# A sparse expert block: the row lookup issued earlier, and other row counts for the gathers

## The chip, the cores and the metric

The kernel runs on one core of a Trainium2 chip. Its time is the device time of one execution in microseconds (us); lower is better. Three executions of the kernel before took 2243.35, 2243.98 and 2247.09 us, median 2243.98 us.

Five engines work side by side, each through its own queue of instructions in order: TensorE (PE in the profile; its weight loads are PEld), VectorE (DVE), ScalarE (ACT), GpSimd (POOL) and SyncE (SP). They wait for one another through semaphores. Transfers run on 16 DMA engines and are issued here by SP (weights) and by POOL (gathers and scatters).

## The reference

One decoder block on 1024 tokens of width 1024. Attention with a forget gate and a gated MLP come first; their merged output goes through a layer norm. Then comes a mixture of 32 experts, which takes most of the time here, and after it a gated embedding and two more norms. Cut to what matters:

```python
x = layer_norm(ALPHA * x + mix)
logits = x @ w_router + b_router            # 1024 x 32
top_val, top_idx = top_k(logits, 4)         # four experts a token
gates = softmax(top_val)
for e in range(32):                         # the rows of x that chose e
    gu = xb @ w_gu[e] + b_gu[e]             # 1024 -> 2048
    gate, up = min(gu[:, :1024], 7), clip(gu[:, 1024:], -7, 7)
    h = (up + 1) * (gate * sigmoid(1.702 * gate))
    y = h @ w_dn[e] + b_dn[e]               # 1024 -> 1024
ffn = sum over a token's four experts of gates * y
x = layer_norm(ALPHA * x + ffn)
```

All inputs are float32. The 4096 assignments spread unevenly over the experts.

## The kernel before, in words

**Row counts.** Experts are ranked by how many tokens chose them. An expert of rank r is given a fixed window of `WIN[r]` rows (lines 35 and 36), filled up with dummy rows; rows beyond a window go through a loop at the end (line 1485). `ORDER` (line 38) is the order in which the ranks are worked on: 32 places, called experts 0 to 31 below, with 120, 92, 232, 102, 98, 180, 114, 88, 256, 100, 128, 192, 118, 128, 150, 156, 124, 144, 164, 124, 134, 208, 108, 128, 176, 126, 138, 168, 120, 130, 160 and 104 rows. A window of over 128 rows is handled in two pieces, of 128 rows and the rest, each with a gather and a scatter of its own.

**The sequence.** Lines 1193 to 1199 write down the work in units, `seq`. Each expert has eight units of the first product: gate and up columns (`"g"`, `"u"`), numbered 0 to 3, in the order g0 g1 u0 u1 g2 g3 u2 u3. Behind the eight units of expert r come the four down-product units (`"d"`) of expert r - 1. So twelve units make a group, and the loop at line 1450 walks through them. Each unit uses 1 MB of float32 weights. For each unit the loop issues:

- the split of a later unit's weights into two half-precision parts: `high` on ScalarE (L1221, four units ahead) and `low` on VectorE (L1227, three units ahead, by the program's order), and then the load of a unit still further ahead on SP (`stage`, L121);
- the unit's own matmuls on TensorE, three for each pair of a 128 x 128 weight block and the rows: `s1` and `columns` (L1318 to L1320), or `s2` for the down product. A down product of at most 128 rows has the rows on the weights' side and 512 columns moving (L1396 to L1400); a wider one goes through `columns` and is transposed back;
- what is due by then from earlier units. `Pipe` (lines 46 to 66) holds these pieces: `p.at(k, f)` runs f at the start of the k-th unit from there.

**The lookup of an expert's rows.** `find(r)` (line 1269) builds a one-hot of the places with eight comparisons on VectorE (`onehot`, L1240). Two units later `pick` multiplies it with token numbers and gate values on TensorE (L1248), eight small matmuls for each 128 rows, and VectorE copies the result (L1250). One unit later `gather` (line 1254) makes the indices with three small VectorE instructions (L1260 to L1262) and issues the indirect DMA on GpSimd (L1265), which brings the rows from DRAM into a tile `xg`.

**The use of the rows.** In the units g2, g3, u2 and u3 of expert r, behind that unit's matmuls, `turn` (line 1280) transposes the rows of expert r + 1 on TensorE (L1288), four transposes each time: one piece in g2 and u2, a second piece in g3 and u3. One unit later ScalarE and VectorE split the result into two halves (L1293, L1294).

**Where the lookup is issued.** `find(r + 3)` stands in unit d0 of expert r (line 1462), the ninth of the twelve units of the group of expert r + 1. The gather goes out at the start of the twelfth unit, and the transposes stand behind the fifth unit of the next group. `find(1)` and `find(2)` are issued ahead of the loop and in its first unit.

**The scatter.** `put` (line 1366) scales an expert's output on ScalarE (L1371) and adds it to the result in DRAM with an indirect DMA on GpSimd (L1374), one or four units into the next group.

**Buffers.** `xg`, the one-hots, the products `z` and the outputs `y` take turns in 16 tiles (`t4`). Weights as loaded, weights as split, `xgT` and `hT` share 15 tiles (`t8`). PSUM's eight banks are handed out in turn too.

Of the kernel before, what the change touches and what calls it, by code (L numbers as in the profile page):

```python
# [30 lines left out]
OFF_V, OFF_U, OFF_GV, OFF_GA, OFF_GB = 1024, 1544, 2056, 2568, 3592  # L31


PICK_TILES, PICK = 4, 26
WIN = [120, 256, 232, 208, 192, 180, 176, 168, 164, 160, 156, 150, 144, 138, 134, 130, 128,
       128, 128, 126, 124, 124, 120, 118, 114, 108, 104, 102, 100, 98, 92, 88]

ORDER = [0, 30, 2, 27, 29, 5, 24, 31, 1, 28, 17, 4, 23, 16, 11, 10, 21, 12, 8, 20, 14, 3, 25, 18, 6, 19, 13, 7, 22, 15, 9, 26]

# [1125 lines left out]
def moe(k, windows, m, p):  # L1165
# [12 lines left out]
    pipe = Pipe()  # L1178
# [36 lines left out]
    def high(n):  # L1215
        if n < len(loads):
            if loads[n][0] == "d" and full(loads[n][1]):
                units[loads[n]] = staged.pop(n)
                return
            units[loads[n]] = k.t8([P, 2, KB // 2, 512], F16, "unit")  # L1220
            nc.scalar.activation(units[loads[n]][:, 0], staged[n], AF.Copy, scale=WS)  # L1221

    def low(n):
        if 0 <= n < len(loads):
            if n in staged:
                u = units[loads[n]]
                nc.vector.scalar_tensor_tensor(u[:, 1], staged.pop(n), WS, u[:, 0], op0=OP.mult, op1=OP.subtract)  # L1227
            stage(n + N_AHEAD)

    def win(r):  # L1230
        return [(w0, min(P, windows[r] - w0)) for w0 in range(0, windows[r], P)]
# [4 lines left out]
    def onehot(r, place):  # L1236
        W = windows[r]
        oh = k.t4([P, NB, 256], F16, "oh")
        for b in range(NB):
            nc.vector.tensor_scalar(oh[:, b, :W], k.iota1[:, :W], place(b), None, op0=OP.is_equal)  # L1240
        return oh

    def pick(r, oh, val):
        out = []
        for w0, n in win(r):
            ps = k.bank()
            for b in range(NB):
                nc.tensor.matmul(ps[:n, :4], oh[:, b, w0:w0 + n], val(b), start=b == 0, stop=b == NB - 1)  # L1248
            t = k.small([P, 4], FT, "slot_t", 4)
            nc.vector.tensor_copy(t[:n], ps[:n, :4])  # L1250
            out.append(t)
        return out
# [16 lines left out]
    def find(r, p):  # L1269

        if r >= R:
            return
        oh = onehot(r, lambda b: k.place[:, b, r:r + 1])

        def second():
            ts = pick(r, oh, lambda b: k.val[:, b, :, r])
            p.at(1, gather, r, ts)
        p.at(2, second)

    def turn(r, w0, n, h, p):  # L1280

        if r not in xgT:
            xgT[r] = k.t8([P, 2, KB, 256], F16, "xgT")
        t, x = xgT[r], xg[r, w0]
        pt = k.bank()
        for j in range(4):
            b = 4 * h + j
            nc.tensor.transpose(pt[:, j * P:j * P + n], x[:n, b * P:(b + 1) * P], k.identf[:n, :n])  # L1288
        src = pt.rearrange("p (j t) -> p j t", j=4)[:, :, :n]
        hi, lo = (t[:, s, 4 * h:4 * h + 4, w0:w0 + n] for s in range(2))  # L1290

        def fin():
            nc.scalar.activation(hi, src, AF.Copy, scale=16.0)  # L1293
            nc.vector.scalar_tensor_tensor(lo, src, 16.0, hi, op0=OP.mult, op1=OP.subtract)  # L1294
        p.at(1, fin)
# [26 lines left out]
    def s1(kind, r, u, p):  # L1322
        un = units.pop((kind, r, u))
        banks = chunks(kind, r, u)
        columns(r, u, un, xgT[r], banks)
        if u % 2:
            p.at(1, take, kind, r, u // 2, banks, p)
# [54 lines left out]
    def s2(r, u, p):  # L1382
        W = windows[r]
        un, h = units.pop(("d", r, u)), hT[r]
        kh = u % 2
        if u == 3:
            del hT[r]
        if W <= P:
            if kh == 0:
                yps[r] = k.bank()  # L1390
            ps = yps[r]
            o = ps[:W]
            for b in range(4):
                kb, start, stop = 4 * kh + b, kh == 0 and b == 0, kh == 1 and b == 3
                if full(r):
                    nc.tensor.matmul(o, h[:, kb, :W], un[:, b], start=start, stop=stop)  # L1396
                    continue
                nc.tensor.matmul(o, h[:, 0, kb, :W], un[:, 0, b], start=start, stop=False)
                nc.tensor.matmul(o, h[:, 0, kb, :W], un[:, 1, b], start=False, stop=False)
                nc.tensor.matmul(o, h[:, 1, kb, :W], un[:, 0, b], start=False, stop=stop)  # L1400
            if kh:
                p.at(1, put, r, 0, W, u // 2, ps)
            return
        banks = chunks("d", r, u)
        columns(r, u, un, h, banks)
        if kh == 0:
            return
        yt = [k.t2([P, 2, 256], FT, "yt") for _ in range(2)]

        def back():  # L1410
            for w0, n in win(r):
                pt = k.bank()
                for c in range(4):
                    nc.tensor.transpose(pt[:n, c * P:c * P + P], yt[c // 2][:, c % 2, w0:w0 + n], k.identf)
                p.at(1, put, r, w0, n, u // 2, pt)

        def out():
            for i in range(2):
                nc.scalar.activation(yt[i][:, :, :W], banks[i][:, :, :W], AF.Copy)
        p.at(1, out)  # L1420
        p.at(3, back)
# [28 lines left out]
    for n, (kind, r, u) in enumerate(seq):  # L1450
        pipe.tick()
        high(n + LEAD)
        if n:
            low(n + LEAD - 1)
        if n >= 30:
            next(over, None)
        if n == len(seq) - TAIL[7]:
            post_rows(k)
        if kind == "d":
            s2(r, u, pipe)  # L1460
            if u == 0:
                find(r + 3, pipe)
        else:
            s1(kind, r, u, pipe)
            if n == 0:
                over = rest()
            if r == 0 and (kind, u) == ("g", 0):
                find(2, pipe)
            if u >= 2 and r + 1 < R:
                i = 2 * (kind == "u") + u - 2  # L1470
                ws = win(r + 1)
                if i % 2 < len(ws):
                    turn(r + 1, *ws[i % 2], i // 2, pipe)
        if n < TAIL[9]:
            step(TAIL[10])
        if n == TAIL[9]:
            p.drain()
# [56 lines left out]
def post_rows(k):  # L1534

    k.bg = row_halves(k, k.a["b_ple_gate"], "bg")
    k.rows = {}
    for n in ("ln2_g", "ln2_b", "ln3_g", "ln3_b"):
        k.rows[n] = k.t4([P, D], FT, n)
        k.row(k.rows[n], k.a[n][0])  # L1540
# [114 lines left out]
@with_exitstack  # L1655
def block_kernel(ctx: ExitStack, tc: tile.TileContext, a: dict, out: bass.AP, dbg=None, phases=9, windows=None):
    ctx.enter_context(tc.manual_schedule())
    k = K(ctx, tc, a, out, dbg)
    windows = [(r, (windows or WIN)[r]) for r in ORDER]
    p = Pipe()  # L1660
    mT, uo = pre(k, p)
    if phases > 1:
        m = mid(k, mT, uo, windows, p)
    if phases > 2:
        us = moe(k, windows, m, p)
    if phases > 3:
        post(k, us, p)
# [24 lines left out]
```

## Time and profile before

| | |
|---|---|
| median of three runs | 2243.98 us |
| lowest, highest | 2243.35, 2247.09 us |
| the profiled execution | 2249.39 us, span 2247.7 us |
| TensorE busy | 2089.9 us, 93% of the span |
| VectorE busy | 1652.9 us, 74% |
| ScalarE busy | 1338.4 us, 60% |
| GpSimd busy | 438.6 us, 20% |
| moved by DMA | 528.77 MB, mean 235 GB/s |
| weights of the experts | 384 loads of 1 MB |
| gathers of rows | 47, 10.0 us median to landing |

The loop over the experts runs from about 764 to 2100 us of the span. A row of the list of instructions in order of time gives the start in us, the duration in us, the engine, the line, the operation, the tiles written and read, the shape and the count, and in brackets the idle time of the engine just before and what ended it. A row of a stretch of time gives the stretch, its length, busy time with the number of instructions in brackets for TensorE, its weight loads, VectorE, ScalarE and GpSimd, then the granted TensorE clock as a share of full speed, the mean busy share of the 16 DMA engines, and GB/s. Spans on GpSimd are rough.

### The profile page before, as it was taken

How to read it: one execution, taken by the hardware profiler on the slowest of the kernel's cores; microseconds unless marked ns; L12 is line 12 of the kernel's file. 1: busy time of each engine (PE TensorE's matmuls, PEld its weight loads, DVE VectorE, ACT ScalarE, POOL GpSimd, SP SyncE). 2: the span in 40 equal slices, each digit the busy share in tenths (PEclk: the TensorE clock that was granted, in tenths of full speed). 3: DMA queues.
4: the chain of work that ended last, by engine and by line, in shares of the span. 5: the costliest groups of instructions: out<-in, count | busy, mean ns of one | idle time of the engine just before them, and what ended most of it. 6: DMA issues, size and time to landing. Idle time of an engine off the chain costs nothing.

```text
span 2247.7 us, 54560 instructions
## 1 busy us (share of the span) xinstructions
PE 2089.9 (93%) x23096; PEld 1692.1 (75%) x23096; DVE 1652.9 (74%) x2705; ACT 1338.4 (60%) x1936; POOL 438.6 (20%) x360
## 2 busy tenths in 40 slices
PE   7999889999999888997999898998999999998596
PEld 6797555444488667977789797998989889998442
DVE  4677666333368786877698798898989888997666
ACT  3324555222111566776688687786978878887443
POOL 1000000000000221203212124221423142341154
PEclk9999999999999999998999999999999999999798
DMA  7201223222224798998989898999989999998621
GB/s 239 67 20 39 68 54 106 58 74 69 92 99 159 264 361 291 316 341 317 336 312 349 271 374 307 335 354 304 358 301 359 351 345 338 354 357 287 222 87 73
DMA packets 285512, 528.77 MB, mean 235 GB/s; under 512 B 16860, under 2 KB 66060, under 8 KB 285264
## 3 DMA queue, kind: packets, MB, share of 16 engines
q1 hardware_dynamic: 263840, 468.29, 59.7%
q0 software_dynamic: 21424, 56.96, 9.3%
q8 instruction: 182, 2.98, 0.5%
q14 instruction: 66, 0.54, 0.1%
HBM read 481.50 MB, written 37.38 MB: 231 GB/s over the span
## 4 chain that ended last, share of the span: by engine, by line
PE 65%; DMA 12%; issue 10%; DVE 6%; POOL 3%; ACT 3%; SPq 1%; ACTq 0%; POOLq 0%; DVEq 0%
PE bank L1318 10%; PE bank L1319 10%; PE bank L1320 10%; DMA xg<-h_dram,slot_i 10%; PE bank L211 3%; PE bank L210 3%; PE bank L209 3%; PE bank L223 3%; PE bank L225 3%; PE bank L224 3%; PE bank L1396 2%; PE bank L1288 1%; DVE unit L1227 1%; POOL rs_t L132 1%; PE bank L835 1%
## 5 line engine op out<-in xcount | busy, mean ns | idle before, releaser
L1227 DVE SCALAR_TENSOR_TENSOR unit<-stage,unit 128x2048 f16<-128x2048 f32 x376 | 853.5, 2283 | 47.3 <-ACT unit L1221 45.8
L1318 PE MATMUL bank<-xgT,unit 128*128 128x128 f16 (+27 forms) x4096 | 758.6, 227 | 0.0
L1320 PE MATMUL bank<-xgT,unit 128*128 128x128 f16 (+27 forms) x4096 | 757.6, 227 | 1.0 <-issue 1.0
L1319 PE MATMUL bank<-xgT,unit 128*128 128x128 f16 (+27 forms) x4096 | 757.9, 227 | 0.1
L1221 ACT ACTIVATE unit<-stage 128x2048 f16<-128x2048 f32 x376 | 715.2, 1910 | 46.0 <-DVE unit L1227 33.5
L1318 PEld LDWEIGHTS <-unit 128*128 128x128 f16 x5056 | 500.4, 99 | 7.1 <-issue 1.7
L1319 PEld LDWEIGHTS <-unit 128*128 128x128 f16 x5056 | 500.1, 99 | 7.0 <-issue 1.6
L1320 PEld LDWEIGHTS <-unit 128*128 128x128 f16 x5056 | 500.0, 99 | 3.0 <-issue 0.5
L1265 POOL DMA_INDIRECT xg<-h_dram,slot_i x47 | 223.8, 4763 | 833.9 <-DVE slot_w L1260 352.2
L1337 ACT ACTIVATE z<-bank,bias 128x128 f32<-128x128 f32 (+27 forms) x512 | 155.6, 376 | 96.3 <-PE bank L1320 92.3
L1318 PE MATMUL bank<-hT,unit 128*128 128x232 f16 (+14 forms) x960 | 208.2, 238 | 0.0
L1320 PE MATMUL bank<-hT,unit 128*128 128x232 f16 (+14 forms) x960 | 208.0, 238 | 0.0
L1319 PE MATMUL bank<-hT,unit 128*128 128x232 f16 (+14 forms) x960 | 208.0, 238 | 0.0
L1294 DVE SCALAR_TENSOR_TENSOR xgT<-bank,xgT 128x512 f16<-128x512 f32 (+12 forms) x94 | 52.2, 556 | 151.0 <-ACT xgT L1293 150.3
L223 PE MATMUL bank<-xT,unit 128*128 128x512 f16 x384 | 145.5, 379 | 2.7 <-DVE pT L62 2.7
L225 PE MATMUL bank<-xT,unit 128*128 128x512 f16 x384 | 145.5, 379 | 1.6 <-DVE unit L104 1.6
L224 PE MATMUL bank<-xT,unit 128*128 128x512 f16 x384 | 145.5, 379 | 0.0
L1374 POOL DMA_INDIRECT acc_dram<-y,slot_i x47 | 120.5, 2564 | 113.0 <-ACT y L1371 100.3
L1288 PE MATMUL bank<-identf,xg 128*128 128x128 f32 (+25 forms) x376 | 54.8, 270 | 65.3 <-DMA xg<-h_dram,slot_i 65.3
L209 PE MATMUL bank<-unit,xT 128*128 128x256 f16 (+1 forms) x384 | 106.3, 277 | 3.3 <-ACT unit L103 3.3
L210 PE MATMUL bank<-unit,xT 128*128 128x256 f16 (+1 forms) x384 | 106.2, 276 | 2.1 <-DVE unit L104 2.1
L742 POOL DMA_DIRECT2D brow<-in_b_out_dram x1 | 0.5, 519 | 545.2 <-DVE unit L104 545.2
(384 smaller groups left out, 3644.9 us busy)
## 6 DMA issues: line engine op xcount, KB each, us to landing
stage<-in_w_gate_up_dram SPq DMA_DIRECT2D x256, 1024.0 KB, 11.1
stage<-in_w_down_dram SPq DMA_DIRECT2D x128, 1024.0 KB, 9.2
stage<-in_w_in_dram SPq DMA_DIRECT2D x22, 512.0 KB, 3.8
stack<-qk_tmp SPq DMA_DIRECT2D x96, 64.0 KB, 2.0
stage<-in_w_in_dram SPq DMA_DIRECT2D x5, 1024.0 KB
xs<-in_x_dram SPq DMA_DIRECT2D x8, 512.0 KB, 9.4
crow<-c_dram SPq DMA_DIRECT2D x8, 512.0 KB, 4.2
stage<-in_w_out_dram SPq DMA_DIRECT2D x4, 1024.0 KB, 5.1
```

Source lines behind the costliest of these rows:

```text
L209: nc.tensor.matmul(ps, lh, rh, start=b == 0, stop=False)
L210: nc.tensor.matmul(ps, lh, rl, start=False, stop=False)
L223: nc.tensor.matmul(box[0], lh, rh, start=b == 0, stop=False)
L224: nc.tensor.matmul(box[0], lh, rl, start=False, stop=False)
L225: nc.tensor.matmul(box[0], ll, rh, start=False, stop=b == n - 1)
L1221: nc.scalar.activation(units[loads[n]][:, 0], staged[n], AF.Copy, scale=WS)
L1227: nc.vector.scalar_tensor_tensor(u[:, 1], staged.pop(n), WS, u[:, 0], op0=OP.mult, op1=OP.subtract)
L1265: nc.gpsimd.indirect_dma_start(out=x[:n], out_offset=None, in_=k.h1d, in_offset=bass.IndirectOffsetOnAxis(ap=i[:n, :1], axis=0))
L1318: nc.tensor.matmul(o, wh, x[:, 0, kb, :W], start=start, stop=False, skip_group_check=True)
L1319: nc.tensor.matmul(o, wh, x[:, 1, kb, :W], start=False, stop=False, skip_group_check=True)
L1320: nc.tensor.matmul(o, wl, x[:, 0, kb, :W], start=False, stop=stop, skip_group_check=True)
L1337: nc.scalar.activation(zs[r][c // 2][:, k0 + c % 2, :W], banks[c // n][:, c % n, :W], AF.Identity, bias=bias_of(r, 4 * v + c + 4 * k0), sc ...
```

## The change

The lookup of expert r + 2 is issued in unit g2 of expert r, the fifth of its group, instead of the ninth (in the old numbering, `find(r + 3)` in d0 of expert r, which belongs to the group of r + 1; both look up the expert two ahead of the group). Expert 2 is still looked up in unit g0 of expert 0. Nine of the 32 windows grow, so that every piece of more than 80 rows has a divisor between 13 and 16; the sum of the windows goes from 4510 to 4538. Rows that are added are dummy rows or rows that went through the loop at the end before.

```diff
 PICK_TILES, PICK = 4, 26
 WIN = [120, 256, 232, 208, 192, 180, 176, 168, 164, 160, 156, 150, 144, 138, 134, 130, 128,
-       128, 128, 126, 124, 124, 120, 118, 114, 108, 104, 102, 100, 98, 92, 88]
+       128, 128, 126, 126, 126, 120, 120, 120, 112, 104, 104, 104, 98, 96, 90]
...
         if kind == "d":
             s2(r, u, pipe)
-            if u == 0:
-                find(r + 3, pipe)
         else:
             s1(kind, r, u, pipe)
             if n == 0:
                 over = rest()
-            if r == 0 and (kind, u) == ("g", 0):
-                find(2, pipe)
+            if (kind, u) == ("g", 2 if r else 0):
+                find(r + 2, pipe)
```

## The prediction

> **What bounds the kernel now.** I read the page first, then the list of waits of TensorE, then the same list cut to the expert loop, then single stretches.
>
> ```profile
> span 2247.7 us, 54560 instructions
> PE 2089.9 (93%) x23096; PEld 1692.1 (75%) x23096; DVE 1652.9 (74%) x2705; ACT 1338.4 (60%) x1936; POOL 438.6 (20%) x360
> PE 65%; DMA 12%; issue 10%; DVE 6%; POOL 3%; ACT 3%; SPq 1%; ACTq 0%; POOLq 0%; DVEq 0%
> ```
>
> TensorE is busy 93% of the span, so what it waits for is what can be won. Its waits, longest first (total us, times, longest), and then its waits on the gathered tile from 1020 to 2060 us alone:
>
> ```profile
> PE bank L1288 <- DMA xg<-h_dram,slot_i: 65.3, 12, 11.3
> PE bank L1584 <- DMA pl<-ple_dram: 22.0, 1, 22.0
> ...
>   DMA xg<-h_dram,slot_i: 53.9, 10
> ```
>
> One wait stands far above the rest: the transposes (L1288) of an expert's rows wait for their gather. 53.9 of the 65.3 us fall on ten experts of the running loop. The other two waits, 11.4 us together, belong to the first two experts. No row shows a wait of TensorE for a weight unit inside the loop; there it stops for gathers alone.
>
> The gathers' issues on GpSimd (start, us, the span on POOL), and the transposes that waited for them, for three experts:
>
> ```profile
> 1012.84 15.01 POOL L1265 DMA_INDIRECT xg<-h_dram,slot_i  x1 [39.40 <-DVE slot_g L1262]
> 1225.85 2.96 POOL L1265 DMA_INDIRECT xg<-h_dram,slot_i  x1 [22.38 <-issue]
> 2009.33 14.30 POOL L1265 DMA_INDIRECT xg<-h_dram,slot_i  x1 [22.64 <-issue]
> ...
> 1035.14 0.85 PE L1288 MATMUL bank<-identf,xg 88*128 88x88 f32 x4 [11.25 <-DMA xg<-h_dram,slot_i]
> 1250.05 1.05 PE L1288 MATMUL bank<-identf,xg 118*128 118x118 f32 x4 [6.81 <-DMA xg<-h_dram,slot_i]
> 2031.82 0.96 PE L1288 MATMUL bank<-identf,xg 104*128 104x104 f32 x4 [7.81 <-DMA xg<-h_dram,slot_i]
> ```
>
> From issue to release these took 1035.14 - 1012.84 = 22.3 us (88 rows), 24.2 us (118 rows) and 22.5 us (104 rows). Without its wait TensorE would have been at the transposes at 1023.9, 1243.2 and 2024.0, so the cover that the order gave was 11.1, 17.4 and 14.7 us. 24.2 us is the longest of the ten.
>
> **What a stall costs beside its idle time.** Eight stretches, the first seven us after a waiting transpose began (the column before the DMA share is the granted clock):
>
> ```profile
> 1035.10:1042.10 7.00, 6.96 (x83) 6.96 (x84) 4.83 (x6) 4.06 (x8) 0.00 (x0) 0.59 0.32 86
> 1250.00:1257.00 7.00, 6.95 (x49) 6.63 (x50) 5.24 (x6) 3.50 (x5) 0.00 (x0) 0.58 0.27 99
> 1372.50:1379.50 7.00, 7.00 (x81) 6.78 (x82) 4.97 (x7) 5.13 (x9) 0.00 (x0) 0.80 0.48 112
> 1416.30:1423.30 7.00, 6.96 (x77) 6.91 (x78) 5.19 (x6) 4.84 (x8) 0.00 (x0) 0.76 1.02 351
> 1541.20:1548.20 7.00, 6.97 (x64) 6.92 (x65) 5.19 (x6) 4.04 (x8) 0.00 (x0) 0.66 0.76 268
> 1666.10:1673.10 7.00, 7.00 (x78) 7.00 (x79) 5.79 (x6) 5.52 (x8) 0.00 (x0) 1.00 0.59 159
> 1828.20:1835.20 7.00, 7.00 (x84) 6.96 (x85) 3.39 (x5) 3.69 (x5) 0.00 (x0) 0.68 0.95 285
> 2031.80:2038.80 7.00, 6.98 (x60) 6.96 (x61) 5.41 (x6) 3.67 (x7) 0.00 (x0) 0.59 0.32 81
> ```
>
> After the longer stalls TensorE runs at a reduced clock. The shortfalls from 1.00 are 0.41, 0.42, 0.20, 0.24, 0.34, 0, 0.32 and 0.41, in sum 2.34; times 7 us that is 16.4 us. I take 15, since matmuls that wait for their weights' load lose less than the clock does.
>
> Do the others use a stall to get ahead? Mostly not. From 850 to 2060 us:
>
> ```profile
> ACT xgT L1293 <- PE bank L1288: 79.3, 31, 10.8
> ...
> DVE xgT L1294 <- ACT xgT L1293: 138.8, 49, 11.9
> ...
> SPq L121 <- PE bank L1288: 131.5, 23, 16.1
> ...
> ACT unit L1221 <- DMA stage<-in_w_gate_up_dram: 4.7, 6, 2.1
> ```
>
> ScalarE's queue has the copy of the transposed rows at its head, VectorE waits for ScalarE, and the weight loads wait for buffers. Everything stops for up to 10.8 to 16.1 us, and everything moves up when the stall goes. ScalarE waited 4.7 us in all for gate and up weights, so the loads have room.
>
> **The change, part by part.**
>
> *The lookup moves up.* Its pieces are eight one-hot comparisons on VectorE, the pick (8 small matmuls per 128 rows on TensorE), three slot operations on VectorE and the indirect DMA on GpSimd. The same work is issued four units of the sequence earlier: the gather goes out behind the eighth unit of a group of twelve instead of the twelfth. So it gains the four down-product units between. These take at least this for a narrow expert (the span, TensorE's busy time and matmuls):
>
> ```profile
> 1265.60:1276.15 10.55, 10.55 (x58) 4.91 (x57) 10.48 (x19) 9.57 (x10) 0.00 (x0) 1.00 0.96 335
> ```
>
> The covers become 11.1 + 10.55 = 21.6, 17.4 + 10.55 = 28.0 and 14.7 + 10.55 = 25.2 us, against landings of 22.3, 24.2 and 22.5. At most 0.7 us would be left, for the first. On POOL's queue the scatters of the previous expert come behind the gather before and after, and nothing is passed; the buffers' rotation keeps its slack, as far as I count the allocations. Removed: 53.9 us of waits and 15 us of slow clock. Bounds: 69.6 us with the first expert's remainder kept, 53.9 + 16.4 = 70.3 us without; where the cover doesn't grow at all is a rival below.
>
> *Where it moves to costs something.* TensorE's pick now stands ahead of the seventh unit, and it waits for the one-hot, which VectorE can start only behind the weight unit it makes in that step. For a narrow expert VectorE is just in time. Group 9 (100 rows), VectorE, then TensorE's two transposes around the sixth and seventh unit, then the one-hot where it stands now; below, VectorE's fourth unit and the transposes ahead of the seventh in group 29, the last with a lookup:
>
> ```profile
> 1153.53 8.89 DVE L1227 SCALAR_TENSOR_TENSOR unit<-stage,unit 128x2048 f16<-128x2048 f32 x4
> 1162.34 0.26 DVE L1354 TENSOR_SCALAR z<-z 128x200 f32<-128x200 f32 x1
> ...
> 1158.47 0.66 PE L1288 MATMUL bank<-identf,xg 128*128 128x128 f32 x4 [0.35 <-DMA xg<-h_dram,slot_i]
> 1163.20 0.62 PE L1288 MATMUL bank<-identf,xg 128*128 128x128 f32 x4
> ...
> 1174.32 1.52 DVE L1240 TENSOR_SCALAR oh<-iota,place 128x192 f16<-128x192 f16 x8
> ...
> 1983.03 2.29 DVE L1227 SCALAR_TENSOR_TENSOR unit<-stage,unit 128x2048 f16<-128x2048 f32 x1 [0.64 <-ACT unit L1221]
> ...
> 1989.72 0.43 PE L1288 MATMUL bank<-identf,xg 32*128 32x32 f32 x4
> ```
>
> VectorE ends its fourth unit at 1162.4, so the one-hot would end at 1162.4 + 1.5 = 1163.9. TensorE reaches the seventh unit halfway between the transposes, near 1161.1, and would wait 2.8 us there. In group 29 (130 rows) the one-hot would end at 1985.3 + 1.4 = 1986.7, and TensorE comes at 1990.1: 3.4 us spare. The same sum between these two, over the 29 groups, is below zero in seven (experts of 88 to 126 rows) and comes to 12.4 us; elsewhere 0.2 to 12.5 us are spare. I take 12.4 as a loss. Its bounds are 0, if a later unit's spare time takes it up, and 29 x 2.8 = 81 us. The wait moves where VectorE is already full, as these stretches of groups 9, 12 and 13 show (third pair: VectorE busy):
>
> ```profile
> 1147.40:1188.30 40.90, 40.55 (x610) 38.15 (x609) 40.59 (x54) 32.35 (x45) 11.15 (x5) 1.00 1.02 369
> 1276.20:1314.30 38.10, 38.10 (x609) 37.99 (x608) 37.86 (x52) 32.23 (x45) 7.58 (x5) 1.00 1.04 372
> 1314.30:1349.40 35.10, 35.10 (x474) 30.73 (x472) 32.44 (x41) 32.43 (x45) 11.98 (x5) 1.00 1.05 366
> ```
>
> VectorE fills 40.59 of 40.90 us in group 9. What it gained in a stall (its queue lost some 2 us less than TensorE did, slow clock included) is gone as well: 3 us more, bounds 0 and 10.
>
> *The row counts* rise by 28 in sum (nine experts). Two units of an 88-row expert and one of a 128-row expert:
>
> ```profile
> 1061.90:1065.70 3.80, 3.80 (x99) 3.80 (x97) 2.50 (x2) 3.80 (x4) 0.00 (x0) 1.00 1.02 395
> 1314.30:1317.00 2.70, 2.70 (x51) 2.69 (x49) 2.70 (x3) 2.23 (x3) 2.70 (x1) 1.00 1.06 391
> ```
>
> (2.70 - 3.80 / 2) / 40 = 0.020 us a column and unit, times 8 units and 28 columns: 4.5 us. A narrow down product has its row count on the weights' side and costs the same. Against that the second expert's gather (92 rows, now 96) may land earlier; its wait is at most 65.3 - 53.9 = 11.4 us with the first one's. VectorE is what follows there, so I take 2 us.
>
> **Sum.** -53.9 - 15 - 2 + 12.4 + 3 + 4.5 = -51.0 us. The profiled execution took 2249.4 us (its span is 2247.7), 5.4 above the median of 2243.98. From the median: 2193 us.
>
> **Rivals.**
> - *TensorE waits for the one-hot in many groups, by a few us.* For it: VectorE is at 99% in groups 9 and 12, and in narrow experts the stalls gave it its small lead. Against it: the wide groups, where its lead is over 10 us. With all 29 sums 2.3 us (one weight unit) worse they come to 33 instead of 12.4 us: 2214 us.
> - *The move is not the cure; the counts are, or neither.* If the issue is not earlier in time, only the counts act. The 118-row gather had a short POOL span of 2.96 us and still took the longest, 24.2 us. The stall at 1250 and these two belong to 118, 124 and 124 rows:
>
> ```profile
> 1416.34 1.09 PE L1288 MATMUL bank<-identf,xg 124*128 124x124 f32 x4 [4.12 <-DMA xg<-h_dram,slot_i]
> 1541.23 1.09 PE L1288 MATMUL bank<-identf,xg 124*128 124x124 f32 x4 [6.11 <-DMA xg<-h_dram,slot_i]
> ```
>
>   The waits fall by at most 6.81 + 4.12 + 6.11 = 17.0 and the clock's part by 7 x (0.42 + 0.24 + 0.34) = 7, so -24 + 4.5 gives 2224 us. By the Trainium skill (DMA: Bandwidth & Descriptors, "Why a DMA increments its semaphore by 16 and not by 1") a transfer is spread over the largest divisor of its row count up to 16, so 118 rows go on two engines and 124 on four; that these were late agrees, that 104 rows (13) took 22.5 us doesn't follow from it.
> - *The spans on POOL grow.* The issues at 1012.84 and 2009.33 took 15.01 and 14.30 us on POOL whatever their rows. If issues beside the second half's VectorE work took 8 us more, landings near 31 us would pass covers of 22 to 28: ten waits of 4 us and 8 us of clock, 2241 us, no change to be told. The Trainium skill (SBUF — State Buffer, "Who interferes with whom") has VectorE and GpSimd share a port pair exclusively, and so speaks for such a wait; the trace shows the long spans, not their cause.
> - *Slower: the pick becomes the loop's own stall.* Place: ahead of the seventh unit of all 29 groups. It decides from 66.4 / 29 = 2.3 us a group, what the rest of the sum gains. At 3 us each, the price in group 9, 87 us are lost: 2244 - 66.4 + 3 + 87 = 2268 us. Against it: 22 of 29 groups have time to spare.
>
> **Chances.** Forecast 0.67, the one-hot's partial wait 0.17, the counts alone 0.06, POOL's spans 0.06, slower 0.04. Within 0.2% (4.5 us) this kernel can't be told from no change. Faster 0.92, same 0.04, slower 0.04. The forecast's own range is 2176 to 2206: both losses at 0 and the clock's part at 16.4 give 2244 - 67.8 = 2176, the lookup's loss doubled gives 2206. Reaching up to the partial wait and the counts alone, the range is 2176 to 2224.
>
> **What would show it.** Right: no row of TensorE waiting on the gathered tile after the second expert, a clock of 1.00 through the loop, and new waits of 1 to 3 us of the pick on the one-hot in narrow groups, near 12 us in sum. If waits on the gather stay at 118 and 124 rows' places only, or everywhere but there, the two halves of the change come apart. Wrong: waits of the pick over 30 us, waits of TensorE for weight units, or of ScalarE for loads well over 10 us, which would mean that the stalls had paid for something I did not see.

## The result, and the profile after

The kernel after takes **2178.24 us** (median, 2177.51 to 2178.93) against 2244.77 us before (median of the runs made beside it): a ratio of 0.970 with an interval of 0.969 to 0.972, or 66.5 us less. Predicted were 2193 us with a range of 2176 to 2224. The profiled execution took 2177.99 us. Between the row counts and the lookup's old place, lines of the kernel stand one further down than before: L1288 is now L1289, L1265 is L1266, L1227 is L1228. Behind that place they stand one further up (L1584 is L1583).

The head of the page after, the first line of its chain, and its group of gathers (busy us and mean ns of one):

```profile
span 2176.3 us, 54567 instructions
PE 2076.7 (95%) x23096; PEld 1681.7 (77%) x23096; DVE 1653.5 (76%) x2705; ACT 1338.9 (62%) x1936; POOL 324.1 (15%) x360
PE 82%; DVE 6%; DMA 3%; ACT 3%; issue 3%; POOL 2%; SPq 1%; ACTq 0%; POOLq 0%; DVEq 0%
L1266 POOL DMA_INDIRECT xg<-h_dram,slot_i x47 | 112.2, 2388 | 477.8 <-DVE slot_g L1263 158.8
```

The span lost 71.4 us (the profiled execution of before was a long one), and TensorE's busy time only 13.2: idle time went, and matmuls at a reduced clock. DMA fell from 12% to 3% of the chain, issue from 10% to 3%. The gathers' spans on POOL add up to 112.2 us.

TensorE's waits after, longest first (us in total, times, longest):

```profile
PE bank L1583 <- DMA pl<-ple_dram: 22.1, 1, 22.1
...
PE bank L1289 <- DMA xg<-h_dram,slot_i: 6.7, 2, 4.0
...
PE bank L1249 <- DVE oh L1241: 1.6, 1, 1.6
```

Two waits on a gathered tile are left of twelve, those of the first two experts, 6.7 us instead of 11.4 for the same two. One new wait of the pick on the one-hot is listed. The three gathers that the prediction followed, in the kernel after (start, us, span on POOL), and the transposes that read them:

```profile
992.80 0.98 POOL L1266 DMA_INDIRECT xg<-h_dram,slot_i  x1 [24.47 <-DVE slot_g L1263]
1195.46 2.98 POOL L1266 DMA_INDIRECT xg<-h_dram,slot_i  x1 [8.49 <-DMA acc_dram<-y,slot_i]
1934.72 3.32 POOL L1266 DMA_INDIRECT xg<-h_dram,slot_i  x1 [8.77 <-PE bank L1321]
```

```profile
1019.41 0.48 PE L1289 MATMUL bank<-identf,xg 90*128 90x90 f32 x4
1226.58 0.58 PE L1289 MATMUL bank<-identf,xg 120*128 120x120 f32 x4
1962.94 0.52 PE L1289 MATMUL bank<-identf,xg 104*128 104x104 f32 x4
```

The covers are now 1019.41 - 992.80 = 26.6, 31.1 and 28.2 us, where the prediction had 21.6, 28.0 and 25.2, and no transpose waits. Landings came forward too. These are the times from issue to landing where the traces give them, for 17 of the 47 gathers before and then for 19 of the 47 after:

```profile
DMA to landing us min/median/max: 6.5/10.0/22.4
```

```profile
DMA to landing us min/median/max: 4.2/8.7/11.2
```

So two things have changed where the stalls were, the cover and the landing. The longest landing on record after, 11.2 us, is about the shortest of the three covers before, 11.1.

The seven us from the start of the first two of these transposes (the column before the DMA share is the granted clock):

```profile
1019.40:1026.40 7.00, 7.00 (x141) 7.00 (x139) 6.93 (x19) 5.31 (x10) 0.00 (x0) 1.00 1.05 387
1226.60:1233.60 7.00, 7.00 (x92) 7.00 (x91) 5.77 (x7) 5.84 (x8) 0.00 (x0) 1.00 1.03 377
```

Before, the same places had a clock of 0.59 and 0.58 and 86 to 99 GB/s. TensorE now gets through 141 and 92 matmuls there instead of 83 and 49, and the weight loads run on. From 850 to 2000 us the granted clock is 1.00 on the average; before, it was 0.97 from 850 to 2050.

Who waits in the loop now, from 850 to 2060 us: VectorE for ScalarE, and the loads' queue for the transposes:

```profile
DVE unit L1228 <- ACT unit L1222: 66.4, 59, 5.1
DVE xgT L1295 <- ACT xgT L1294: 51.9, 26, 6.2
```

```profile
SPq L122 <- PE bank L1289: 105.5, 25, 9.3
```

VectorE waits 51.9 us for the transposed rows instead of 138.8, and the queue of the loads stands for the transposes at most 9.3 us at a time instead of 16.1.

### The profile page after: what moved, and what is told of

Same layout as the page of the kernel before. It is cut to its first block, busy times and chain, and to the rows that moved or that the text cites. A ratio compares the mean times of both kernels' runs of the same rounds, so it can differ in the third digit from the quotient of the medians.

```text
span 2176.3 us, 54567 instructions
## 1 busy us (share of the span) xinstructions
PE 2076.7 (95%) x23096; PEld 1681.7 (77%) x23096; DVE 1653.5 (76%) x2705; ACT 1338.9 (62%) x1936; POOL 324.1 (15%) x360
## 4 chain that ended last, share of the span: by engine, by line
PE 82%; DVE 6%; DMA 3%; ACT 3%; issue 3%; POOL 2%; SPq 1%; ACTq 0%; POOLq 0%; DVEq 0%
PE bank L1319 14%; PE bank L1320 14%; PE bank L1321 14%; PE bank L211 4%; PE bank L210 4%; PE bank L212 4%; PE bank L224 3%; PE bank L226 3%; PE bank L225 3%; PE bank L1397 2%; PE bank L1399 2%; PE bank L1401 2%; PE bank L1400 2%; PE bank L1289 2%; DVE unit L1228 1%
## 5 line engine op out<-in xcount | busy, mean ns | idle before, releaser
L1228 DVE SCALAR_TENSOR_TENSOR unit<-stage,unit 128x2048 f16<-128x2048 f32 x376 | 854.8, 2284 | 69.4 <-ACT unit L1222 69.0
L1319 PE MATMUL bank<-xgT,unit 128*128 128x120 f16 (+22 forms) x4096 | 753.4, 225 | 0.0
L1320 PE MATMUL bank<-xgT,unit 128*128 128x120 f16 (+22 forms) x4096 | 753.1, 225 | 0.0
L1321 PE MATMUL bank<-xgT,unit 128*128 128x120 f16 (+22 forms) x4096 | 753.0, 225 | 0.0
L1222 ACT ACTIVATE unit<-stage 128x2048 f16<-128x2048 f32 x376 | 714.8, 1911 | 38.9 <-DVE unit L1228 25.4
L1338 ACT ACTIVATE z<-bank,bias 128x120 f32<-128x120 f32 (+22 forms) x512 | 156.9, 379 | 100.6 <-PE bank L1321 98.0
L1266 POOL DMA_INDIRECT xg<-h_dram,slot_i x47 | 112.2, 2388 | 477.8 <-DVE slot_g L1263 158.8
L210 PE MATMUL bank<-unit,xT 128*128 128x256 f16 (+1 forms) x384 | 106.0, 276 | 3.0 <-ACT unit L104 3.0
L211 PE MATMUL bank<-unit,xT 128*128 128x256 f16 (+1 forms) x384 | 105.9, 276 | 2.1 <-DVE unit L105 2.1
L105 DVE SCALAR_TENSOR_TENSOR unit<-stage,unit 128x1024 f16<-128x1024 f32 (+2 forms) x38 | 62.4, 1673 | 58.8 <-ACT unit L104 58.7
L212 PE MATMUL bank<-unit,xT 128*128 128x256 f16 (+1 forms) x384 | 105.8, 275 | 0.0
L1295 DVE SCALAR_TENSOR_TENSOR xgT<-bank,xgT 128x512 f16<-128x512 f32 (+7 forms) x94 | 52.1, 554 | 62.4 <-ACT xgT L1294 60.4
```

Of the source, the lines that this page charges most:

```text
L210: nc.tensor.matmul(ps, lh, rh, start=b == 0, stop=False)
L211: nc.tensor.matmul(ps, lh, rl, start=False, stop=False)
L212: nc.tensor.matmul(ps, ll, rh, start=False, stop=b == n - 1)
L1319: nc.tensor.matmul(o, wh, x[:, 0, kb, :W], start=start, stop=False, skip_group_check=True)
L1320: nc.tensor.matmul(o, wh, x[:, 1, kb, :W], start=False, stop=False, skip_group_check=True)
L1321: nc.tensor.matmul(o, wl, x[:, 0, kb, :W], start=False, stop=stop, skip_group_check=True)
```

## The experiments

The theory to be tested: the earlier issue gives cover, and cover is what removed the stalls; the row counts hardly matter beyond the columns that they add. The rivals: the counts do it; the new place does it by short POOL spans; the pick's wait is only hidden by chance.

**The two halves apart.** *move_only* is the kernel after with the counts of before, *counts_only* the kernel before with the counts of after.

```
 move_only (from after)       counts_only (from before)
-  126, 126, 126, 120, 120,   -  126, 124, 124, 120, 118,
-  120, 112, 104, 104, 104,   -  114, 108, 104, 102, 100,
-  98, 96, 90]                -  98, 92, 88]
+  126, 124, 124, 120, 118,   +  126, 126, 126, 120, 120,
+  114, 108, 104, 102, 100,   +  120, 112, 104, 104, 104,
+  98, 92, 88]                +  98, 96, 90]
```

> The changed kernel with the row counts of before (126, 124, 124, 120, 118, 114, 108, 104, 102, 100, 98, 92, 88 at the end of the list). Theory 'the earlier issue is the cure': no wait of the transposes on the gather after the second expert; 28 columns less are 4.5 us won, the second expert's wait goes back from 2.8 to about 7 us, so 2173 to 2183 us. Rival 'the counts are the cure, the move only adds': the waits at the 118-, 124- and 124-row experts (17 us and 7 us of clock before) stay in part, with others: 2195 us or more. Whichever holds, the gathers' POOL spans tell which part made them fall from 223.8 to 112.2 us.

> The kernel before with the row counts of after; the lookup stays three experts ahead in the first down unit. Theory 'the earlier issue is the cure': waits of 35 to 50 us on the gather stay, only some of those at 118 and 124 rows go, 4.5 us of columns are added: 2220 to 2245 us. Rival 'the counts are the cure': most waits go, 2185 to 2195 us.

*move_only* took 2197.61 us and *counts_only* 2220.98, beside 2245.15 for the kernel before: ratios of 0.978 (0.975 to 0.980) and 0.989 (0.987 to 0.992). So the move alone wins 47.5 us and the counts alone 24.2; on top of the move the counts win 2197.61 - 2178.24 = 19.4. The first theory's figure for the move alone (2173 to 2183) was 14.6 us too low even at its upper end; its figure for the counts alone held at its edge. The rival had the move's time right, and its reason wrong, as TensorE's waits in *move_only* show:

```profile
PE bank L1289 <- DMA xg<-h_dram,slot_i: 11.6, 2, 7.6
...
PE bank L1400 <- DVE unit L1228: 4.9, 2, 2.4
PE bank L1249 <- DVE oh L1241: 4.4, 5, 2.4
```

No transpose of the loop waits for its gather: the move does cure those. Instead the down product (L1400) waits for a weight unit, and behind that wait stands ScalarE, which waits for a load (group 14, 1332 to 1378 us of *move_only*):

```profile
ACT unit L1222 <- DMA stage<-in_w_down_dram: 13.1, 2, 9.3
```

From 850 to 2060 us ScalarE waits 52.3 us for weights in *move_only* and 7.4 us in the kernel after. The pick waits for its one-hot as well, 4.4 us in five waits.

Where the time sits is seen from the groups' lengths (us, from the first gate matmul of an expert to that of the next; rows with two numbers have them before/after):

| group | rows | before | counts alone | move alone | after |
|---|---|---|---|---|---|
| 0 and 1 | 120, 92/96 | 74.4 | 69.9 | 79.6 | 74.1 |
| 6 | 114/120 | 50.2 | 48.4 | 36.4 | 37.0 |
| 9 | 100/104 | 40.9 | 41.4 | 43.8 | 42.3 |
| 11 | 192 | 52.9 | 43.1 | 43.1 | 43.1 |
| 14 | 150 | 46.4 | 46.6 | 46.2 | 37.6 |
| 15 | 156 | 46.7 | 40.7 | 40.7 | 40.7 |
| 18 | 164 | 50.1 | 41.5 | 43.0 | 41.5 |
| 19 | 124/126 | 38.5 | 38.8 | 42.3 | 38.8 |
| 25 | 126 | 46.2 | 46.6 | 38.9 | 38.9 |
| 30 | 160 | 49.8 | 47.6 | 39.0 | 39.0 |

The counts alone cure groups 11, 15 and 18, where the 118- and the two 124-row experts are transposed: 9.8 + 6.0 + 8.6 = 24.4 us of the 32.0 by which these two profiled spans differ. The move takes most of the stall out of those and out of 6, 25 and 30. Group 14 needs both: it stalled for a gather before, and with the move alone for weights. With the move alone, groups 0 and 1, 19, 18 and 9 also stay longer than after, by 5.5, 3.5, 1.5 and 1.5 us.

**One count.** Is it one expert's count, and its gather or its scatter? *one118* is the kernel after with 118 instead of 120 rows for the 13th expert in the loop's order (its own group is 12). In *one118_gather120* the gather of that expert still fetches 120, so only the scatter has 118.

```
 one118
-       128, 128, 126, 126, 126, 120, 120, 120, 112, 104, 104, 104, 98, 96, 90]
+       128, 128, 126, 126, 126, 120, 118, 120, 112, 104, 104, 104, 98, 96, 90]
 one118_gather120: this, and the gather's row count of its own
+GATHER = {118: 120}
+    def gwin(r):
+        return [(0, GATHER.get(windows[r], windows[r]))] if r and windows[r] <= P else win(r)
...
-        for w0, n in win(r):
+        for w0, n in gwin(r):
```

> The changed kernel with one row count put back: the 13th expert in the loop's order has 118 rows instead of 120, gathered and scattered. Theory 'two DMA engines carry 59 rows each, at 0.33 us a row some 20 us, and the weight loads stand behind them': the group two behind it (14) takes about 8.6 us longer, as in the run with all the old counts, 2178 + 8.6 - 0.3 = 2186 us. Rival 'the loss of that run came from all thirteen old counts together': 2178 to 2180 us.

> As the run with one count of 118, but the gather of that expert fetches 120 rows (two of them unused), so that only its scatter has 118. Theory 'the scatter does it, because it goes out with four weight units of a 128-row expert to load behind it, while the gather's 26 us stay under its cover of 31': 2186 us again. Rival 'the gather does it, by holding the weight loads': 2178 to 2180 us.

They took 2186.51 and 2186.33 us (ratios 0.973, 0.971 to 0.975, and 0.973, 0.971 to 0.976), where 2186 was expected of each. One count of two rows less costs 8 us, and the scatter alone costs all of it; group 14 takes 45.9 and 44.7 us, where it takes 37.6 in the kernel after. In the second run the scatter goes out at 1325.6 us, and from 1324 to 1369 us ScalarE waits for down weights as it did in *move_only*:

```profile
ACT unit L1224 <- DMA stage<-in_w_down_dram: 11.8, 2, 9.4
```

The transfers of *one118_gather120* from 1344 to 1364 us (busy share of 16 DMA engines in tenths, and GB/s, in 40 slices of 0.5 us):

```profile
DMA  2211111111796999999841155999999999989999
GB/s 70 70 37 25 29 37 33 25 29 37 98 98 213 389 401 377 389 422 401 270 135 37 33 98 107 385 410 397 410 401 414 410 393 377 389 225 360 406 406 397
```

For 4 us (1345 to 1349) the mean busy share of the DMA engines is 0.14, near two of sixteen (0.125), and they move 31 GB/s instead of some 390, while TensorE is busy all the time. In these 4 us 21 packets of the queue of gathers and scatters pass and 20 of the queue of weight loads. That fits a scatter on two engines and weight units that lack only these two engines' share; that the other fourteen have nothing left to do is argued from it. The longest time from issue to landing is that of this scatter in *one118_gather120*, whose trace has the landings of all 47 scatters (the next is 12.1 us); below it the kernel after, with 15 of 47:

```profile
DMA to landing us min/median/max: 5.5/10.5/31.0
```

```profile
DMA to landing us min/median/max: 7.9/10.0/11.2
```

31.0 us for 59 rows on each of two engines are 0.53 us a row, the turns of the weight loads included. In the kernel after no landing on record is over 11.2 us. The Trainium skill (DMA: Bandwidth & Descriptors, "Why a DMA increments its semaphore by 16 and not by 1") has a transfer run on the largest divisor of its row count up to 16. The share of 0.14 fits it: 118 is 2 x 59, so two engines.

**All counts prime.** *primes* gives the thirteen narrow experts behind the first 127, 113, 107, 101 or 97 rows; *primes_gather* has these counts in the gathers alone, *primes_scatter* in windows and scatters, with gathers of 128, 120, 112 or 104 rows.

```
 primes
-  126, 126, 126, 120, 120, 120, 112, 104, 104, 104, 98, 96, 90]
+  127, 127, 127, 127, 127, 127, 113, 107, 107, 107, 101, 97, 97]
 primes_gather: the counts of after, and
+  GATHER = {126: 127, 120: 127, 112: 113, 104: 107, 98: 101, 96: 97, 90: 97}
 primes_scatter: the counts of primes, and
+  GATHER = {127: 128, 113: 120, 107: 112, 101: 104, 97: 104}
```

> The changed kernel with prime row counts in the thirteen narrow gathers below the 120-row first one (127 six times, 113, 107, 107, 107, 101, 97, 97: 45 columns more, so 45 x 8 x 0.020 = 7.2 us of TensorE). Theory 'the lead covers any spread': waits on the gather stay at the first two experts and the time is 2178 + 7 = 2185 us, somewhat less where TensorE waits for VectorE anyway. Rival 'the counts carry part of the gain': gathers and scatters of a prime count take so much longer (24.2 us before with 118 rows against covers of 27 to 41 us after) that some wait again: over 2195 us.

> The changed kernel whose narrow gathers after the first fetch a prime number of rows (127, 113, 107, 101 or 97; the rows past the window are not used), while products and scatters keep the counts of after. With both gathers and scatters prime the run before this took 2573 us, of which 96.7 us are waits on the gather. Theory 'one DMA engine carries all rows of a prime count at 0.33 us a row (127 rows landed after 42 us) and the weight loads that need this engine queue behind it': gathers and scatters do about equal harm, so 2330 to 2430 us, with landings of 32 to 42 us. Rival 'only the landing of the gather itself counts, it passes the cover by 6 to 15 us in eight groups and the rest came from the scatters': about 2178 + 97 + 20 of slow clock, 2270 to 2300 us. Rival 'the prime gathers are covered and the scatters do all the harm': under 2200 us.

> The primes kernel (windows of 127, 113, 107, 101 and 97 rows, so prime scatters) whose narrow gathers fetch 128, 120, 112 or 104 rows instead, the rows past the window unused. Theory 'gathers and scatters do about equal harm through the weight loads': 2330 to 2430 us, with no wait of the transposes on the gather after the second expert, and TensorE waiting for weight units. Rival 'the gather's landing does the harm': 2185 to 2200 us (the 45 columns alone are 7 us).

*primes* took 2572.98 us (1.145, 1.142 to 1.148), 395 more than after and 328 more than before, for 45 columns that cost 7. No expectation had thought of such a loss. *primes_gather* took 2333.18 (1.040, 1.038 to 1.042) and *primes_scatter* 2520.57 (1.123, 1.121 to 1.125). So prime gathers cost 155 us, at the lower end of what was expected, and prime scatters 335 beyond their columns, which is more than was expected and not the equal harm of the theory. Apart they cost more than the 395 us of both together. In *primes_gather* the waits of TensorE on gathers make up most of the loss: 122.5 us in eleven, where the kernel after has 6.7 in two.

A 127-row gather of *primes_gather*, then the transpose that waits for it, then the transfers from 1264 to 1304 us (slices of 1 us):

```profile
1252.29 4.46 POOL L1271 DMA_INDIRECT xg<-h_dram,slot_i  x1 [8.59 <-DMA acc_dram<-y,slot_i]
```

```profile
1296.66 1.06 PE L1294 MATMUL bank<-identf,xg 120*128 120x120 f32 x4 [13.15 <-DMA xg<-h_dram,slot_i]
```

```profile
DMA  9999999999854499999210000000005999999996
GB/s 312 349 357 341 359 363 363 305 240 272 264 191 70 131 399 399 371 371 346 86 47 29 25 25 25 29 25 25 25 25 82 393 399 350 406 401 373 403 352 72
```

The gather takes 44.4 us, or 0.35 us for each of 127 rows on the average. Its cover was 1296.66 - 13.15 - 1252.29 = 31.2 us. From 1285 to 1294 us the mean busy share of the DMA engines is 0.06, one of sixteen, at 25 GB/s; TensorE stands still then, so part of this lull is the stall itself. So cover alone isn't enough; it is enough for gathers that run on many engines. The prime scatters are slower still (the landings of *primes_scatter*), and TensorE's waits there are not on gathers behind the first two experts:

```profile
DMA to landing us min/median/max: 7.9/11.0/62.2
```

```profile
PE bank L1420 <- ACT yt L1425: 124.7, 12, 20.0
PE bank L1588 <- DVE h L164: 64.4, 3, 62.6
...
PE bank L1294 <- DMA xg<-h_dram,slot_i: 7.3, 2, 3.8
```

Behind these waits stands ScalarE again: from 850 to 2200 us it waits 349.0 us for weights. The longest single wait, 62.6 us, belongs to the step behind the loop, which reads what the scatters add up; VectorE waits 48.7 us for that read, where it waits 14.7 in the kernel after. 62.2 us for 127 rows are 0.49 us a row against the gather's 0.35. Why a row of the accumulating scatter takes longer was not tested.

**How far must the counts go?** *lean* raises only those that by the divisors would run on four engines or fewer (and 100 to 104), and keeps 114, 108, 102 and 88.

```
-  126, 126, 126, 120, 120, 120, 112, 104, 104, 104, 98, 96, 90]
+  126, 126, 126, 120, 120, 114, 108, 104, 102, 104, 98, 96, 88]
```

> The changed kernel with only the counts below 6 engines raised: 92 to 96, 118 to 120, 124 to 126 twice (and 100 to 104, where VectorE is short); 114, 108, 102 and 88 stay as before (6, 12, 6 and 11 engines). 14 columns less are 14 x 8 x 0.020 = 2.2 us. Theory 'six engines are enough, since 19 rows each at 0.33 us take 6.3 us': 2175 to 2178 us, no new wait. Rival 'only divisors of 13 to 16 keep the weight loads running': 2180 to 2190 us, with longer groups one and two behind the 114- and 102-row experts.

It took 2177.47 us (0.969, 0.967 to 0.971). That is 0.8 us below the kernel after and can't be told from it. The groups one and two behind the 114- and 102-row experts are as long as in the kernel after, within 0.1 us, so divisors of 6 keep the loads running here as 13 to 16 do, and the total shows no loss at 11 and 12. The longest scatter of *lean*, that of 114 rows, lands after 15.2 us:

```profile
DMA to landing us min/median/max: 5.5/10.3/15.2
```

**Cover or place?** The gathers' POOL spans halved with the move: 118.0 us in *move_only*, but in *counts_only*

```profile
L1265 POOL DMA_INDIRECT xg<-h_dram,slot_i x47 | 224.0, 4766 | 813.2 <-DVE slot_w L1260 309.1
```

with these waits of TensorE for a gather from 1020 to 2060 us:

```profile
PE bank L1288 <- DMA xg<-h_dram,slot_i: 33.0, 7, 9.6
```

So the move might work by the place, not the lead. *far* keeps the old place and the new counts, and looks up four experts ahead instead of three; its slot tables have 11 buffers instead of 10.

```
             if u == 0:
-                find(r + 3, pipe)
+                find(r + 4, pipe)
...
-            if r == 0 and (kind, u) == ("g", 0):
-                find(2, pipe)
+            if r < 2 and (kind, u) == ("g", 2 * r):
+                find(2 + r, pipe)
```

> The kernel before with the row counts of after, and the lookup at its old place in the first down unit, but four experts ahead instead of three (the slot tables get 11 buffers instead of 10). The gathers keep the neighbours that made their POOL spans long (224 us in sum) and gain a whole group, 33 us or more, of cover. Theory 'the cover is what counts': the waits on the gather in the loop (35 of 40.4 us in the run with the counts alone) go although the POOL spans stay near 224 us, and the time is 2175 to 2190 us. Rival 'the place counts, because GpSimd gets its issues through quickly there': waits stay, 2210 us or more. Rival 'a gathered tile that is held a group longer takes its buffer from others': no wait on the gather, but new waits for buffers, 2195 us or more.

It took 2184.69 us (0.973, 0.971 to 0.976). TensorE's waits, and the gathers' group on its page:

```profile
PE bank L1288 <- DMA xg<-h_dram,slot_i: 7.1, 2, 3.8
```

```profile
L1265 POOL DMA_INDIRECT xg<-h_dram,slot_i x47 | 264.5, 5628 | 699.7 <-DVE slot_g L1262 333.5
```

The gathers take even longer on POOL, and no transpose of the loop waits. Beside *counts_only*, which takes 36.3 us more, this shows that cover is enough to cure the stalls, whatever POOL does. It doesn't show that the kernel after needed all of its cover: there the landings are shorter too, and no run has the short landings with the old cover. The 6.4 us above the kernel after sit in groups 2, 3 and 7 (1.2, 3.8 and 1.3 us longer); for what, no run tells.

**Other places.** *place_u0* looks up two units earlier than after, *place_u2* two later.

```
-            if (kind, u) == ("g", 2 if r else 0):
+            if (kind, u) == (("u", 0) if r else ("g", 0)):     # place_u0
+            if (kind, u) == (("u", 2) if r else ("g", 0)):     # place_u2
```

> The changed kernel with the lookup two units earlier, at the first up unit (pick ahead of the fifth unit, gather behind the sixth). Theory 'after the change no stall is left that a longer cover could take': no gain from the cover; pick waits may change by a few us: 2174 to 2186 us. Rival 'there are late gathers that only the trace of one run hid': more than 5 us faster. The POOL spans of the gathers (112.2 us in sum at this place, 224.0 at the old one) show whether the place alone sets them.

> The changed kernel with the lookup two units later, at the third up unit (pick ahead of the ninth unit, gather behind the tenth), 5 to 8 us less cover than after. Theory 'landings of 4 to 11 us leave most of the cover of 27 to 41 us unused': still no wait on the gather in the loop, and VectorE's margins at the pick are larger or smaller by a few us: 2174 to 2184 us. Rival 'the POOL spans grow again next to the down product, and landings of 20 us and more come back': waits in groups where the cover falls to 20 us, 2190 us or more.

They took 2181.76 (0.972, 0.971 to 0.974) and 2189.27 us (0.976, 0.974 to 0.977). Neither has a gather's wait in the loop, so the longer cover bought nothing, as expected. The later place loses 11 us, more than the theory had, and not by late landings: 6.1 of them are in group 9, 3.2 in group 22 and 3.0 in group 2. The gathers' groups of *place_u0* and *place_u2*:

```profile
L1266 POOL DMA_INDIRECT xg<-h_dram,slot_i x47 | 64.8, 1378 | 257.6 <-DVE slot_g L1263 70.0
```

```profile
L1266 POOL DMA_INDIRECT xg<-h_dram,slot_i x47 | 86.8, 1846 | 664.0 <-DVE slot_g L1263 176.6
```

Of *place_u2*'s 11 us, TensorE's list gives 3.2 to the pick:

```profile
PE bank L1249 <- DVE oh L1241: 3.2, 2, 2.8
```

The rest is not accounted for by a listed wait.

**The pick's wait.** *onehot2* makes the eight comparisons twice.

```
-        for b in range(NB):
+        for b in 2 * list(range(NB)):
             nc.vector.tensor_scalar(oh[:, b, :W], k.iota1[:, :W], place(b), None, op0=OP.is_equal)
```

> The changed kernel with the eight comparisons of the one-hot made twice, the second time over the first (1.0 to 1.5 us more of VectorE a lookup, about 1.4 on the average). Theory of the prediction 'the pick is just in time in narrow groups, VectorE has no lead there': seven sums already below zero grow by 1.4 each and VectorE, 97 to 99% busy there, keeps the loss: 10 to 20 us more, 2188 to 2198 us. Rival 'TensorE has its own slack before the pick and VectorE catches up inside the group': by the margins measured after (one-hot's end to the pick's start 0 to 2.5 us in nine groups), only these wait, 0.2 to 1.6 us each: 4 to 9 us more, 2182 to 2187 us.

It took 2186.47 us (0.974, 0.972 to 0.976): 8.2 us more, for 1694.0 - 1653.5 = 40.5 us more of VectorE's busy time. That is in the rival's band and below the theory's. A fifth of the extra work reaches the end, so VectorE has slack at the new place in most groups, and little to spare in some.

## Why the prediction was right, and where it was wrong

The time was in the range and 15 us below the number, and the forecast's own case happened: the gathers' waits went. But the terms of the counts were wrong by 21.9 us, and the losses at the pick came only in part. That the range held was in part luck: its lower end, 2176 us, came from both losses at 0 and the clock's part at 16.4, not from a gain of the counts, and the time came out 2.2 us above it.

- **Gather waits, -53.9, and clock, -15.** Right for the kernel after: no transpose of the loop waits, and the clock is 1.00 where it was 0.59. The covers came out 3.0 to 5.0 us longer than worked out. What would be late next was wrong. The prediction let "everything move up when the stall goes". *move_only* shows that the move alone does not get there: in group 14 the stall for the gather was replaced by one for weights, and *one118_gather120* shows that the 118-row scatter is enough for it. The step "the loads have room" was read from a profile in which the stalls gave them that room: with the same counts ScalarE waited 4.7 us for gate and up weights before and 34.3 us in *move_only*. Waits of ScalarE for loads well over 10 us are the sign that the prediction had named for this. The scatters were put aside because they stand behind the gather on POOL's queue; what they do in the DMA engines' queues was not costed.
- **The row counts, +4.5, and the second expert, -2.** This is the step that failed. It priced the counts in TensorE's columns, and in one gather. They are worth -19.4 us on top of the move and -24.2 alone, columns included. For the case without the move, the rival "the counts alone act" had worked out 2224 us from the three stalls at 118 and 124 rows; 2220.98 were measured, at those three places. A piece was there and was not put into the sum: by the divisors the 118-row scatter has the same 59 rows an engine as the gather that took 24.2 us. Its own landing is not in the trace of before. The longest of the 30 that are is this one, of a 100-row scatter that went out at 1229.1 us, some 3 us behind that gather, and landed at 1250.9, when the gather's wait had just ended:

```profile
DMA to landing us min/median/max: 6.5/11.1/21.8
```

- **The pick's wait, +12.4.** Mis-sized. One wait of 1.6 us is listed, in group 1. The prediction shows the rows of two of its 29 sums, for groups 9 and 29. In group 9, VectorE and then TensorE in the kernel after:

```profile
1134.20 8.89 DVE L1228 SCALAR_TENSOR_TENSOR unit<-stage,unit 128x2048 f16<-128x2048 f32 x4
1143.01 1.52 DVE L1241 TENSOR_SCALAR oh<-iota,place 128x192 f16<-128x192 f16 x8
```

```profile
1143.33 1.79 PE L1249 MATMUL bank<-val,oh 128*128 128x4 f16 x16
```

  The one-hot ends at 1144.53, 1.2 us behind the start of the pick, and the pick's sixteen small matmuls stretch over 1.79 us beside it. 2.8 were predicted. VectorE is just in time, as predicted, but it ends its fourth unit 13.7 us into the group, where it had taken 15.0 before. With the counts of before the price was nearly met: in *move_only* group 9 is 2.9 us longer than before, and with the new counts (104 rows instead of 100) 0.9 longer than in *counts_only*. Over all groups *move_only* lists only 4.4 us of such waits, but in group 9 it lists 0.6 of the 2.9 us, so the whole price with the old counts is not known. Why VectorE is earlier than it was is not shown.
- **The lost lead, +3.** No sign of it in the totals: VectorE waits 66.4 us for ScalarE in the loop (the row above), so mostly it is not the one that is late.
- **The sum.** With the counts at -19.4 instead of +2.5, and the move at -47.5 where its four terms had -53.5, the difference is -21.9 + 6.0 = -15.9, close to the 15 us by which the forecast missed. The two errors in the move, losses at the pick that came only in part and weight stalls that were not seen, work against each other and leave the 6.0.
- **The rivals.** That POOL's spans grow is refuted for this place (112.2 us) and beside the point: with 264.5 us (*far*) nothing waits. That the pick becomes the loop's stall did not happen; at *place_u2* and in *onehot2* it begins to. That the prediction gave the counts 2 us of gain in its likeliest case was its real weakness. The Trainium skill's rule on divisors, which it quoted beside the rival, is borne out by the runs with 118 and 127 rows; that it doesn't explain the 104 rows that took 22.5 us stands too. Those had 14.30 us on POOL. A long span there goes with a late landing even for few rows: before, a second piece of 10 rows had 14.1 us on POOL (at 1809.1) and landed after 19.1.

## What to carry to other kernels

A gather or scatter with an awkward row count costs twice: by its own landing, and by keeping a DMA engine or two busy that every large load needs as well, so count rows per DMA engine (rows divided by the largest divisor up to 16) for scatters as for gathers, and look for slices in which the DMA share falls to one or two sixteenths. When a long stall is removed, ask which transfers used the stall to finish; a profile with stalls can't show that they have room. A change of two parts should be priced as each part alone and both together, since here one stall (group 14) needed both.

## What the runs showed of the hardware beyond that

- From issue to landing one DMA engine took 0.35 us a row of 4 KB in the gathers (44.4 us for 127 rows) and 0.49 to 0.53 us in the accumulating scatters (62.2 us for 127 rows, 31.0 for 59 an engine). Near the end of these, all transfers together fell from some 390 to 25 and 31 GB/s.
- On such an engine gathers or scatters and weight loads took turns. From 1286 to 1294 us of *primes_gather*, at a busy share of one engine, 33 packets of the queue of gathers and scatters (4 KB each) and 33 of the queue of weight loads (2 KB each) passed, 0.24 us a pair.
- The span of an indirect DMA on POOL differs with the order of the work around it: the same 47 gathers, with the same row counts, took 264.5, 224.0, 112.2, 86.8 and 64.8 us in sum in *far*, *counts_only*, the kernel after, *place_u2* and *place_u0*. The cause was not tested.
